# Binding the S5 work of a step behind that step's gate passes, and giving the v steps more of it than the z_b steps

## The chip, the cores and the metric

The kernel runs on one core of one Trainium2 chip. The metric is the device time of one execution in microseconds; lower is better. The engines are TensorE (PE, matrix products into PSUM), VectorE (DVE), ScalarE (ACT), GpSimd (POOL), and SyncE (SP), whose queue issues the DMAs. Each engine runs its own list of instructions in the order in which it was written down when the kernel was compiled.

## The reference

One layer of a bidirectional encoder trunk over a prompt of 1024 positions and a sample of 2048, width 1024, all in float32:

```
h = rmsnorm(x) ;  u, v, z_a, x_b, z_b = split(h @ w_in)          # 5 x 1024 columns
# branch A: gated MLP over chunks of 128 positions, 4 heads of 256
vh  = layernorm(gelu(v))
sv  = einsum('hpq,ncqhd->ncphd', w_s, vh) + b_s                  # 128 x 128 mixing
y_a = gelu(u) * sv * silu(z_a)
# branch B: S5, 64 groups of 16 channels, 64 complex states, forward and backward
s_t = a * s_(t-1) + B x_t ;  y = Re(C s) + d_skip * x            # scans over time
gy  = gelu(y) ;  y_b = gy * sigmoid(gy @ w_glu + b_glu) * silu(z_b)
out = rmsnorm(x + concat(y_a, y_b) @ w_out)
```

## The kernel before, in words

Every large product is made of three matmuls (`mm3`, lines 59 to 61), since each operand is held as a rounded high part and a low rest. Making the two parts is a `split`: a copy on ScalarE, then a subtraction on VectorE or GpSimd. The positions are worked on in three blocks of 1024 (`th`), each in two halves (`jh`).

The kernel has a first stage (norm, x_b columns, S5 tables), a middle stage, and a last one (the GLU product and the output projection). The change lies in the middle stage. There, for each block in the order 2, 0, 1, come three loops of *steps*. A step is one half's product with one slab of weights, and its *gate*, the passes that empty its PSUM bank:

- 16 **v steps** (`v_part`): 48 matmuls of 256 columns, then, in every second of them, a Gelu on ScalarE; for the odd column blocks also batch statistics on VectorE (L507).
- 16 **z_b steps** (`zb_op`): 24 matmuls of 512 columns, then a tanh on ScalarE (L527) and a multiply on VectorE (L528). Beside them stand 8 small matmuls of the position mixing (`mix`, tile `sv`, L484 and L485), their two passes (L488, L489), and the normalisation and split of the next chunk of v (`norm_chunk` L465, `split_chunk` L472 and L473).
- 32 **u and z_a steps** (`u_op`, `za_op`): 24 matmuls of 512 columns each; u has a Gelu on ScalarE (L566) and two passes on VectorE (L563, L568), z_a a tanh (L527) and two passes on VectorE (L528, L577).

PSUM holds five banks under the tag `mm`; the products of all three kinds and `sv` share them. The weights of a sweep of two steps (tile `whl`) are double buffered; in the first block they are split on ScalarE (L151) and GpSimd (L152) and written to DRAM, in the other two they are loaded again from there.

After each step the program calls `advance`, which adds 0.5 to a counter `done[0]` and takes from the generator `s5_groups` as many *half groups* of the S5 branch as 128 x `done[0]` / 92 asks for (`TOT` is 92, of 96 in all; the S5 work ends eight units of counter before the middle stage does). The two halves of a group g are:

- the first, `states(g)`: 6 matmuls (tile `pb`), two products with the tables (L1094, L1095), two sums, two scans over time (L1102, tile `gt`), two products (L1107, L1108), two sums (L1109, L1110), the split of `h` (ScalarE copy and VectorE subtraction, L1036 and L1037). Then the splits for group g+1 (`prepare`) and, for even g, the first part of two groups' tables (`tables`), for odd g the last part (`finish_tables`: a VectorE pass L1055, an abs L1056 and a sine L1058 on ScalarE). The sine lies in another table of ScalarE's functions than tanh and Gelu, so that a table load stands on either side of it.
- the second: `outputs(g-1)`: 9 matmuls (tile `py`) and a Gelu (L1127); `decay(g+1)`, a ScalarE pass that writes the factor `dec` of the next group's scan (L1116) into its only buffer; `issue(g+2)`, the loads of a later group on SP's queue.

The order in which each engine runs its instructions is not the order of the source. A planner works it out at compile time with a model of durations: of the instructions that its model finds ready it takes the one with the highest priority, and priority goes by the place in the source, with `tc.high_priority` moving the gates ahead by 100 places. So it may set S5 work that the source places after a step ahead of that step's gate, where the model finds the engine free.

Of the kernel before, what the change touches and what calls it, by code (L numbers as in the profile page):

```python
# [24 lines left out]
J = 8  # L25
NTH = 3
KK = NTH * P
GRP = 64
# [35 lines left out]
def hybrid_encoder(ctx, tc, a, outs):  # L64
# [117 lines left out]
    def sweep(pool, half, ops, after, hp=WHP):  # L182

        ws = [ready.pop(0) for _ in ops]
        for jh in range(2):
            for w, f in zip(ws, ops):
                ps = pool.tile([P, 512], F32, tag="mm", name="mm")
                h = half(jh)
                for kt in range(KT):
                    mm3(nc, ps, w[:, 0, kt], w[:, 1, kt], h[kt][:, 0], h[kt][:, 1], kt == 0, kt == KT - 1)  # L190
                if jh:
                    next_w(hp)
                f(jh, ps)
                after()
# [5 lines left out]
    def cols(t):  # L200
        return t.rearrange("p (k j) -> p j k", j=J)
# [161 lines left out]
    with ExitStack() as p2:  # L363
# [5 lines left out]
        ps_mm = p2.enter_context(tc.tile_pool(name="ps_mm2", bufs=5, space=PSUM, reuse_waits="tile"))  # L369
        ps_b = p2.enter_context(tc.tile_pool(name="ps_b", bufs=1, space=PSUM))  # L370

        s5 = s5_groups(nc, spool, ps_b, small, kio, f8h, f8l, r8, xb_d, ks_d, mat_d, gy_d)
        done = [0, 0]
        wg, g0 = [], []

        def stage_tile(name):
# [24 lines left out]
                    g0.append((gf, gh))  # L401

        late = [[], []]

        def flush():

# [4 lines left out]
        def advance(n=0.5):  # L411

            flush()
            done[0] += n
            if done[1] == 2 * GRP and done[0] % 1 == 0:
                preload()
            while done[1] < min(2 * GRP, 2 * GRP * done[0] / TOT):
                next(s5)
                done[1] += 1

        def get_half(hf):
# [15 lines left out]
        for th in (2, 0, 1):  # L437
# [53 lines left out]
            def v_part(acc, w, cb, q, jh):  # L491

                for cc in range(2):
                    ps = acc[jh][cc]
                    for i in range(2):
                        csl = slice(P * (2 * cc + i), P * (2 * cc + i) + P)
                        for t in range(4):
                            h, wh, wl = hs[jh][4 * q + t], w[:, 0, 2 * t:2 * t + 2], w[:, 1, 2 * t:2 * t + 2]

                            mm3(nc, ps[:, i], h[:, 0, csl], h[:, 1, csl], wh, wl, q == t == i == 0, q == i == 1 and t == 3)  # L500
                    if q:
                        c = slice(2 * cc, 2 * cc + 2)
                        sl = slice(256 * cb, 256 * cb + 256)
                        with tc.high_priority(offset=HP):
                            S.activation(vs[jh][:, c, sl], ps, AF.Gelu_apprx_tanh)
                            for i in (2 * cc, 2 * cc + 1) if cb % 2 else ():
                                V.bn_stats(sts[jh][:, i, cb // 2], vs[jh][:, i, 512 * (cb // 2):256 * cb + 256])  # L507
                advance()

            for cb in range(4):  # L510
                acc = [[ps_mm.tile([P, 2, 256], F32, tag="mm", name="acc") for _ in range(2)] for _ in range(2)]
# [12 lines left out]
            def gate(t, jh, ps):  # L524

                o = by_j(t, jh)
                S.activation(o, cols(ps), AF.Tanh, scale=0.5)  # L527
                V.scalar_tensor_tensor(o, o, 1.0, cols(ps), op0=ALU.add, op1=ALU.mult)  # L528

            def store(dst, fb, t):  # L530
                x = dst[J * th:J * th + J, :, fb].rearrange("j p k -> p j k"), t
# [7 lines left out]
            def zb_op(fb, jh, ps):  # L539
                if not jh:  # L540
                    mix(fb, 0)
                    if fb < KT - 1:
                        norm_chunk(fb + 1)
                        split_chunk(fb + 1, 0)
                    zs[0] = stage_tile("zb").rearrange("p (j k) -> p j k", j=J)
                with tc.high_priority(offset=HP):
                    gate(zs[0], jh, ps)
                if jh:
                    mix(fb, 1)
                    if fb < KT - 1:  # L550
                        split_chunk(fb + 1, 1)
                    store(zb_d, fb, zs[0])

            for fb in range(KT):
                sweep(ps_mm, lambda jh: hs[jh], [lambda *x: zb_op(fb, *x)], advance)

            def part(fb, jh):
                return vs[jh][:, :, P * fb:P * fb + P]

            def u_op(fb, jh, ps):  # L560
                t = part(fb, jh)
                with tc.high_priority(offset=HP):
                    V.scalar_tensor_tensor(t, t, LG[:, fb:fb + 1], RB[:, fb:fb + 1].to_broadcast([P, 4, P]),  # L563
                                           op0=ALU.mult, op1=ALU.add)
                with tc.high_priority(offset=HP):
                    S.activation(ps, ps, AF.Gelu_apprx_tanh)  # L566
                    t = t.rearrange("p c (j k) -> p c j k", j=J)
                    V.tensor_tensor(t, t, ps.rearrange("p (c k j) -> p c j k", c=4, j=J), op=ALU.mult)  # L568

            def za_op(fb, jh, ps):  # L570
                if not jh:
                    zs[1] = stage_tile("za").rearrange("p (j k) -> p j k", j=J)
                with tc.high_priority(offset=HP):
                    gate(zs[1], jh, ps)
                    o = by_j(zs[1], jh)
                    o = o.rearrange("p j (c k) -> p j c k", c=4)
                    V.tensor_tensor(o, o, part(fb, jh).rearrange("p c (j k) -> p j c k", j=J), op=ALU.mult)  # L577
                if jh:
                    store(ya_d, fb, zs[1])
                    if th != 1 and fb == KT - 1:  # L580
                        hs[1] = get_half((2 * th + 3) % 6)
                elif th != 1 and fb == KT - 1:
                    hs[0] = get_half((2 * th + 2) % 6)
# [429 lines left out]
    finish(*last)  # L1013


def s5_groups(nc, sp, ps, small, kio, f8h, f8l, r8, xb_d, ks_d, mat_d, gy_d):


    V, S, G, T = nc.vector, nc.scalar, nc.gpsimd, nc.tensor
    dma = nc.sync.dma_start  # L1020
    sh = [P, 2, KK]
# [11 lines left out]
        V.memset(keep[64:128, c:c + 1], 0.0)  # L1033

    def split(t, src, eng):
        S.copy(t[:, 0], src)  # L1036
        eng.tensor_tensor(t[:, 1], src, t[:, 0].bitcast(F32), op=ALU.subtract)  # L1037

    def tables(g):

# [42 lines left out]
    def states(g):  # L1083
        u, mi, mo = st[g]
        tb = st.pop(("tab", g))
        cs = tb[:, 0:1].to_broadcast(sh)
        sn = tb[:, 1:2].to_broadcast(sh)

        pb = ps.tile([P, 2, 512], F32, tag="pb", name="pb")[:, :, 0:KK]
        for i in range(2):  # L1090
            mm3(nc, pb[:, i], mi[:, 0, i], mi[:, 1, i], u[:, 0], u[:, 1], True, True)
        b1 = sp.tile(sh, F32, tag="b1", name="b1")
        b2 = sp.tile(sh, F32, tag="b2", name="b2")
        V.tensor_tensor(b1, pb, cs, op=ALU.mult)  # L1094
        V.tensor_tensor(b2, pb[:, ::-1], sn, op=ALU.mult)  # L1095
        V.tensor_tensor(b1[:, 0], b1[:, 0], b2[:, 0], op=ALU.add)
        V.tensor_tensor(b1[:, 1], b1[:, 1], b2[:, 1], op=ALU.subtract)
        dec = st.pop(("dec", g))
        bf = b1.rearrange("p i k -> p (i k)")
        for r, o, z in ((slice(0, 64), gp[:, 2:2 * KK + 2], (0, P)), (slice(64, 128), gp[:, 0:2 * KK], (P - 1, KK - 1))):  # L1100
            f = slice(None, None, 1 if r.start == 0 else -1)
            V.tensor_tensor_scan(o[r, f], dec[r, f], bf[r, f], 0.0, op0=ALU.mult, op1=ALU.add)  # L1102
            V.memset(gt[r, :, z[0]:z[1] + 1:z[1] - z[0]], 0.0)
        h = sp.tile([P, 2] + sh[1:], F32R, tag="h", name="h", bufs=2)
        h1 = sp.tile(sh, F32, tag="b1", name="h1")
        h2 = sp.tile(sh, F32, tag="b2", name="h2")
        V.tensor_tensor(h1, gt, cs, op=ALU.mult)  # L1107
        V.tensor_tensor(h2, gt[:, ::-1], sn, op=ALU.mult)  # L1108
        V.tensor_tensor(h1[:, 0], h1[:, 0], h2[:, 0], op=ALU.subtract)  # L1109
        V.tensor_tensor(h1[:, 1], h1[:, 1], h2[:, 1], op=ALU.add)  # L1110
        split(h, h1, V)
        st[g] = u, mo, h

    def decay(g):
        dec = sp.tile([P, 2 * KK], F32, tag="dec", name="dec")
        S.activation(dec.rearrange("p (i k) -> p i k", i=2), keep.unsqueeze(1).to_broadcast(sh), AF.Copy,  # L1116
                     scale=r8[:, g:g + 1])
        st["dec", g] = dec
# [25 lines left out]
    for g in range(GRP):  # L1144
        states(g)
        store()
        if g < GRP - 1:
            prepare(g + 1)
        if g % 2 == 0 and g < GRP - 2:
            tables(g + 2)  # L1150
        if g % 2 == 1 and g < GRP - 1:
            finish_tables(g + 1)
        yield
        if g:
            outputs(g - 1)
        if g < GRP - 1:
            decay(g + 1)
        if g < GRP - 2:
            issue(g + 2)
        if g == GRP - 1:  # L1160
            store()
            outputs(g)
            store()
        yield
# [30 lines left out]
```

## Time and profile before

| | |
|---|---|
| time, median of 3 runs | 2592.8 us (2588.3 to 2597.44) |
| the profiled execution | 2590.47 us |
| its span, first to last instruction | 2588.7 us |
| TensorE busy | 2465.0 us |
| VectorE, ScalarE, GpSimd busy | 1745.0, 999.5, 608.2 us |
[...]

The span is of one execution with the hardware profiler on. A busy TensorE is one with a matmul in flight; lower clock shows as longer matmuls, not as idle time. The middle stage's steps run from about 398 to 1783 us of the span: the first block's v, z_b and u/z_a from 398.5, 504.0 and 649.9 us, the z_b of the other two from 994.9 and 1454.0.

### The profile page before, as it was taken

Reading aid. Unit: us, or ns where it says so; the run is one execution under the profiler, and the core shown is the slowest. Engines: PE = TensorE matmul, PEld = TensorE weight load, DVE = VectorE, ACT = ScalarE, POOL = GpSimd, SP = SyncE. Lnnn points to the kernel's source line nnn. Section 1 sums busy time; section 2 is a strip of 40 time slices with the busy share of each in tenths; the row PEclk is TensorE's granted clock in tenths of the full one; section 3 lists DMA queues with packets and bytes.
Section 4 is the critical chain, followed back from the end, with each engine's and each line's share of the span. In section 5 each row is a group of like instructions: output and inputs, shape, how many; then the busy total and the mean of one; then the engine's idle time right before and its main releaser. Section 6 shows DMA issues by size and latency. Waiting matters only on the chain.

```text
span 2588.7 us, 34059 instructions
## 1 busy us (share of the span) xinstructions
PE 2465.0 (95%) x12313; PEld 2090.5 (81%) x12313; DVE 1745.0 (67%) x2890; ACT 999.5 (39%) x1729; POOL 608.2 (23%) x623
## 2 busy tenths in 40 slices
PE   6899999998999799999989989999999999999998
PEld 4777779877887698888879978888888888888887
DVE  6888857888988888888887989874344433333332
ACT  5343344455445444545444354422223311111110
POOL 1579863434322312211021221001000200000000
PEclk9999999999999899999999999999999999999999
DMA  8565554434554533444453344446565732222220
GB/s 233 168 190 145 148 159 168 165 120 153 166 172 148 188 125 124 128 132 132 147 171 121 125 130 133 132 146 195 148 183 152 228 110 95 97 94 98 98 74 33
DMA packets 363017, 367.21 MB, mean 142 GB/s; under 512 B 40768, under 2 KB 308576, under 8 KB 350560
## 3 DMA queue, kind: packets, MB, share of 16 engines
q1 hardware_dynamic: 311008, 343.99, 41.9%
q10 hardware_dynamic: 51840, 21.04, 3.4%
q8 instruction: 97, 1.59, 0.3%
q14 instruction: 72, 0.59, 0.1%
HBM read 229.76 MB, written 135.20 MB: 141 GB/s over the span
## 4 chain that ended last, share of the span: by engine, by line
PE 57%; DVE 20%; ACT 4%; DMA 3%; issue 3%; POOL 2%; SPq 0%; ACTq 0%; DVEq 0%; POOLq 0%
PE mm L59 15%; PE mm L60 15%; PE mm L61 15%; DVE gt L1102 4%; PE acc L61 3%; PE acc L59 3%; PE acc L60 3%; DVE h L1108 1%; DVE h L1107 1%; DVE b L1095 1%; DMA whl<-wc_d 1%; DMA hf<-hs_d 1%; DVE u L1037 1%; DVE tab L1048 1%; DVE b L1094 1%
## 5 line engine op out<-in xcount | busy, mean ns | idle before, releaser
L59 PE MATMUL mm<-w,yh 128*128 128x512 f32 x768 | 302.5, 394 | 0.0
L60 PE MATMUL mm<-w,yh 128*128 128x512 f32 x768 | 301.9, 393 | 0.0
L61 PE MATMUL mm<-w,yh 128*128 128x512 f32 x768 | 301.3, 392 | 0.0
L59 PE MATMUL mm<-ha,whl 128*128 128x512 f32 x704 | 281.2, 400 | 18.1 <-ACT whl L151 10.3
L61 PE MATMUL mm<-ha,whl 128*128 128x512 f32 x704 | 278.0, 395 | 2.5 <-POOL whl L152 2.3
L59 PE MATMUL mm<-hb,whl 128*128 128x512 f32 x704 | 278.5, 396 | 0.0
L60 PE MATMUL mm<-ha,whl 128*128 128x512 f32 x704 | 278.0, 395 | 0.0
L60 PE MATMUL mm<-hb,whl 128*128 128x512 f32 x704 | 276.7, 393 | 0.0
L61 PE MATMUL mm<-hb,whl 128*128 128x512 f32 x704 | 276.5, 393 | 0.0
L152 POOL TENSOR_TENSOR whl<-wf,whl 128x512 fp32r<-128x512 f32 x112 | 168.4, 1519 | 272.7 <-ACT whl L151 258.5
L1102 DVE TENSOR_TENSOR_SCAN gt<-dec,b 64x768 f32<-64x768 f32 x128 | 229.9, 1796 | 3.8
L1116 ACT ACTIVATE dec<-keep,r 128x768 f32<-128x768 uint8 x64 | 60.1, 938 | 314.2 <-DVE gt L1102 314.2
L59 PEld LDWEIGHTS mm<-ha,whl 128*128 128x128 f32 x704 | 134.3, 191 | 47.5 <-ACT whl L151 12.0
L61 PEld LDWEIGHTS mm<-w,yh 128*128 128x128 f32 x768 | 144.2, 188 | 33.9
L59 PEld LDWEIGHTS mm<-w,yh 128*128 128x128 f32 x768 | 144.2, 188 | 33.3
L60 PEld LDWEIGHTS mm<-w,yh 128*128 128x128 f32 x768 | 144.0, 187 | 33.0
L681 DVE SCALAR_TENSOR_TENSOR yh<-yf,yh 128x512 fp32r<-128x512 f32 x96 | 66.8, 699 | 146.7 <-ACT yh L680 96.8
L1037 POOL TENSOR_TENSOR mo<-m,mo 128x384 fp32r<-128x384 f32 x64 | 79.0, 1234 | 366.9 <-ACT mo L1036 358.5
L61 PEld LDWEIGHTS mm<-ha,whl 128*128 128x128 f32 x704 | 134.1, 191 | 33.5 <-POOL whl L152 5.3
L710 DVE TENSOR_TENSOR xr<-xr,mm 128x512 f32<-128x512 f32 x48 | 33.0, 687 | 183.8 <-PE mm L61 183.8
L61 PEld LDWEIGHTS mm<-hb,whl 128*128 128x128 f32 x704 | 133.7, 190 | 28.2
L60 PEld LDWEIGHTS mm<-ha,whl 128*128 128x128 f32 x704 | 134.4, 191 | 26.7 <-DVE ha L285 1.1
(242 smaller groups left out, 6026.3 us busy)
## 6 DMA issues: line engine op xcount, KB each, us to landing
whl<-wc_d SPq DMA_DIRECT2D x64, 1024.0 KB
wc_d<-whl SPq DMA_DIRECT2D x32, 1024.0 KB
wf<-in_w_in_dram SPq DMA_DIRECT2D x112, 256.0 KB
m<-mat_d SPq DMA_DIRECT2D x128, 128.0 KB
xb_d<-xo SPq DMA_DIRECT2D x24, 512.0 KB
U<-xb_d SPq DMA_DIRECT2D x64, 192.0 KB
gy_d<-gy SPq DMA_DIRECT2D x64, 192.0 KB
zb_d<-zb SPq DMA_DIRECT2D x24, 512.0 KB
```

Of the source, the lines that this page charges most:

```text
L59: nc.tensor.matmul(out, lh, rh, start=first, stop=False)
L60: nc.tensor.matmul(out, lh, rl, start=False, stop=False)
L61: nc.tensor.matmul(out, ll, rh, start=False, stop=last)
L152: G.tensor_tensor(flat[:, 1, sl], wf, flat[:, 0, sl].bitcast(F32), op=ALU.subtract)
L681: V.scalar_tensor_tensor(y[:, 1], yf, sc, y[:, 0].bitcast(F32), op0=ALU.mult, op1=ALU.subtract)
L710: V.tensor_tensor(x, x, t.ps[i], op=ALU.add)
L1037: eng.tensor_tensor(t[:, 1], src, t[:, 0].bitcast(F32), op=ALU.subtract)
L1048: V.scalar_tensor_tensor(fr, kio, f8l[:, g + q:g + q + 1], fr, op0=ALU.mult, op1=ALU.add)
L1094: V.tensor_tensor(b1, pb, cs, op=ALU.mult)
L1095: V.tensor_tensor(b2, pb[:, ::-1], sn, op=ALU.mult)
L1102: V.tensor_tensor_scan(o[r, f], dec[r, f], bf[r, f], 0.0, op0=ALU.mult, op1=ALU.add)
L1116: S.activation(dec.rearrange("p (i k) -> p i k", i=2), keep.unsqueeze(1).to_broadcast(sh), AF.Copy, scale=r8[:, g:g + 1])
```

## The change

Three things are done. First, each gate pass is remembered in a dictionary `tail`, one entry for ScalarE and one for VectorE, and every S5 half group that `advance` takes is traced inside `tc.issue_after` of these entries: its instructions on ScalarE come in ScalarE's list after the last gate pass traced there, and likewise on VectorE. Such an edge is an order in one engine's list and no wait on a semaphore. Second, inside the S5 generator `decay(g+1)` is bound in the same way behind the ScalarE copy of the split of `h` of group g. Third, `advance` is called with 0.66 after a v step and 0.34 after a z_b step; a u or z_a step keeps 0.5. The later preloads for the last stage are counted by calls instead of by whole units, which gives the same every second call.

```
+        tail = {}
...
             flush()
             done[0] += n
-            if done[1] == 2 * GRP and done[0] % 1 == 0:
+            done[2] += 1
+            if done[1] == 2 * GRP and done[2] % 2 == 0:
                 preload()
             while done[1] < min(2 * GRP, 2 * GRP * done[0] / TOT):
-                next(s5)
+                with ExitStack() as behind:
+                    for i in tail.values():
+                        behind.enter_context(tc.issue_after(i.ins))
+                    next(s5)
                 done[1] += 1
...
-                            S.activation(vs[jh][:, c, sl], ps, AF.Gelu_apprx_tanh)
+                            tail["S"] = S.activation(vs[jh][:, c, sl], ps, AF.Gelu_apprx_tanh)
...
-                advance()
+                advance(0.66)
...
-                S.activation(o, cols(ps), AF.Tanh, scale=0.5)
-                V.scalar_tensor_tensor(o, o, 1.0, cols(ps), op0=ALU.add, op1=ALU.mult)
+                tail["S"] = S.activation(o, cols(ps), AF.Tanh, scale=0.5)
+                tail["V"] = V.scalar_tensor_tensor(o, o, 1.0, cols(ps), op0=ALU.add, op1=ALU.mult)
...
-                sweep(ps_mm, lambda jh: hs[jh], [lambda *x: zb_op(fb, *x)], advance)
+                sweep(ps_mm, lambda jh: hs[jh], [lambda *x: zb_op(fb, *x)], lambda: advance(0.34))
...
+                    tail["S"] = S.activation(ps, ps, AF.Gelu_apprx_tanh)
+                    tail["V"] = V.tensor_tensor(t, t, ps.rearrange("p (c k j) -> p c j k", c=4, j=J), op=ALU.mult)
+                    tail["V"] = V.tensor_tensor(o, o, part(fb, jh).rearrange("p c (j k) -> p j c k", j=J), op=ALU.mult)
...
-        split(h, h1, V)
+        st["hi"] = split(h, h1, V)
...
         if g < GRP - 1:
-            decay(g + 1)
+            with tc.issue_after(st["hi"].ins):
+                decay(g + 1)
```

## Rows read from the trace of the kernel before

**Rows 1.** The page, busy time of TensorE: us, share of the span, instructions.

```profile
PE 2465.0 (95%) x12313; PEld 2090.5 (81%) x12313; DVE 1745.0 (67%) x2890; ACT 999.5 (39%) x1729; POOL 608.2 (23%) x623
```

**Rows 2.** Windows by stage: length, PE, PEld, DVE, ACT, POOL busy, granted clock.

```profile
398.50:504.00 105.50, 105.10 (x841) 104.64 (x840) 85.20 (x111) 49.12 (x80) 38.46 (x29) 1.00 0.52 176
504.00:649.90 145.90, 127.07 (x595) 108.85 (x594) 131.58 (x188) 78.15 (x142) 59.75 (x44) 0.93 0.44 140
649.90:877.70 227.80, 211.59 (x936) 175.68 (x934) 200.98 (x245) 111.48 (x180) 69.88 (x54) 0.97 0.51 165
...
994.90:1122.40 127.50, 121.70 (x596) 104.95 (x594) 110.88 (x187) 68.53 (x123) 34.44 (x28) 0.96 0.41 129
...
1454.00:1582.00 128.00, 118.30 (x598) 102.09 (x597) 113.98 (x172) 63.39 (x116) 32.75 (x27) 1.00 0.41 126
```

**Rows 3.** Windows of three stretches of the second block: v, z_b, u/z_a.

```profile
915.40:994.94 79.54, 79.54 (x637) 79.54 (x637) 62.00 (x92) 35.95 (x57) 7.91 (x8) 1.00 0.35 117
1015.88:1059.47 43.59, 43.59 (x223) 37.88 (x223) 36.19 (x63) 25.96 (x48) 12.51 (x10) 1.00 0.44 137
1205.95:1295.32 89.37, 89.37 (x413) 76.20 (x412) 73.89 (x104) 42.08 (x62) 8.37 (x9) 1.00 0.44 139
```

**Rows 4.** Waits of TensorE, 398 to 1783 us: total us, times, longest.

```profile
PE sv L484 <- DVE zb L528: 19.3, 9, 5.0
PE mm L59 <- ACT whl L151: 10.3, 4, 6.5
...
PE sv L484 <- ACT vh L472: 6.1, 2, 4.3
```

**Rows 5.** Waits of ScalarE, the same stretch.

```profile
ACT dec L1116 <- DVE gt L1102: 314.2, 61, 12.2
...
ACT h L1036 <- DVE h L1110: 87.6, 48, 5.0
```

**Rows 6.** Waits of VectorE, the same stretch.

```profile
DVE za L528 <- ACT za L527: 44.5, 15, 5.7
...
DVE v L568 <- ACT mm L566: 37.6, 14, 4.6
DVE zb L528 <- ACT zb L527: 30.1, 9, 4.8
```

**Rows 7.** Timeline of ScalarE from 606.5 us, a z_b step: start, duration.

```profile
610.62 0.94 ACT L1116 ACTIVATE dec<-keep,r 128x768 f32<-128x768 uint8 x1 [7.06 <-DVE gt L1102]
611.47 0.58 ACT L527 ACTIVATE zb<-mm 128x512 f32<-128x512 f32 x1
```

**Rows 8.** Timeline of TensorE at the same step.

```profile
613.02 0.57 PE L484 MATMUL sv<-wsT,vh 128*128 128x256 f32 x1 [4.10 <-DVE v L489]
```

**Rows 9.** Timeline of ScalarE from 743 us, a z_a step.

```profile
751.24 0.85 ACT L1056 ACTIVATE tab<-tab 128x768 f32<-128x768 f32 x1 [3.50 <-DVE tab L1055]
...
753.40 1.58 ACT L1058 ACTIVATE tab<-tab,qpi 128x1536 f32<-128x1536 f32 x1
755.00 1.28 ACT L527 ACT_TABLE_LOAD   x1
756.30 0.60 ACT L527 ACTIVATE za<-mm 128x512 f32<-128x512 f32 x1
```

**Rows 10.** Timeline of VectorE at the same step.

```profile
756.93 0.69 DVE L528 SCALAR_TENSOR_TENSOR za<-za,mm 128x512 f32<-128x512 f32 x1 [4.85 <-ACT za L527]
```

**Rows 11.** Groups of VectorE, second block's u/z_a stage: total us, mean ns.

```profile
L1107 DVE TENSOR_TENSOR h<-gt,tab 128x768 f32<-128x768 f32 x11 | 10.5, 958 | 0.3
...
L1110 DVE TENSOR_TENSOR h<-h,h 128x384 f32<-128x384 f32 x11 | 6.9, 624 | 0.0
```

**Rows 12.** Groups of VectorE, first v stage.

```profile
L507 DVE BATCH_NORM_STATS2 st<-v 128x6 f32<-128x512 f32 x14 | 9.1, 684 | 3.2 <-ACT v L505 3.2
```

**Rows 13.** One line's instructions, a table pass: ns least, median, most.

```profile
L1048 DVE SCALAR_TENSOR_TENSOR tab<-kio,f8l,tab x64: 558/614/1655, 378.1 to 1666.0; 128x384 f32<-128x384 f32 x64
```

**Rows 14.** Timeline of VectorE from 546 us, a z_b step.

```profile
546.66 5.10 DVE L465 TENSOR_SCALAR v<-v,rvy,nb 128x1024 f32<-128x1024 f32 x3
```

More of the change, by code (lines that the diff above doesn't have):

```diff
@@ L370, in hybrid_encoder @@
         ps_b = p2.enter_context(tc.tile_pool(name="ps_b", bufs=1, space=PSUM))
-        s5 = s5_groups(nc, spool, ps_b, small, kio, f8h, f8l, r8, xb_d, ks_d, mat_d, gy_d)
-        done = [0, 0]
+        s5 = s5_groups(tc, spool, ps_b, small, kio, f8h, f8l, r8, xb_d, ks_d, mat_d, gy_d)
+        done = [0, 0, 0]
         wg, g0 = [], []
@@ L565, in u_op @@
                 with tc.high_priority(offset=HP):
-                    S.activation(ps, ps, AF.Gelu_apprx_tanh)
+                    tail["S"] = S.activation(ps, ps, AF.Gelu_apprx_tanh)
                     t = t.rearrange("p c (j k) -> p c j k", j=J)
-                    V.tensor_tensor(t, t, ps.rearrange("p (c k j) -> p c j k", c=4, j=J), op=ALU.mult)
+                    tail["V"] = V.tensor_tensor(t, t, ps.rearrange("p (c k j) -> p c j k", c=4, j=J), op=ALU.mult)
             def za_op(fb, jh, ps):
@@ L576, in za_op @@
                     o = o.rearrange("p j (c k) -> p j c k", c=4)
-                    V.tensor_tensor(o, o, part(fb, jh).rearrange("p c (j k) -> p j c k", j=J), op=ALU.mult)
+                    tail["V"] = V.tensor_tensor(o, o, part(fb, jh).rearrange("p c (j k) -> p j c k", j=J), op=ALU.mult)
                 if jh:
@@ L1013, in s5_setup, with s5_groups @@
     finish(*last)
-def s5_groups(nc, sp, ps, small, kio, f8h, f8l, r8, xb_d, ks_d, mat_d, gy_d):
+def s5_groups(tc, sp, ps, small, kio, f8h, f8l, r8, xb_d, ks_d, mat_d, gy_d):
+    nc = tc.nc
     V, S, G, T = nc.vector, nc.scalar, nc.gpsimd, nc.tensor
@@ L1035, in split @@
     def split(t, src, eng):
-        S.copy(t[:, 0], src)
+        hi = S.copy(t[:, 0], src)
         eng.tensor_tensor(t[:, 1], src, t[:, 0].bitcast(F32), op=ALU.subtract)
+        return hi
     def tables(g):
```

## The prediction

> **What bounds the kernel now.** I read the page first: TensorE is busy for 2465.0 of 2588.7 us, so 124 us are to be had in all [rows 1]. The windows by stage then say where those 124 us lie. The projections of the middle stage run from 398 to 1783 us, in three blocks of 64 steps: 16 v steps, 16 z_b steps, 32 u/z_a steps. To know what a stage would take if TensorE never waited, I looked for stretches in which its busy time equals the window and the clock is 1.00 [rows 3]. The first holds 12 v steps and 4 S5 groups (12x48 + 4x15 = 636 matmuls, 637 counted): 6.63 us a step. The second holds 6 z_b steps and 2 groups: 7.27 us. The third holds 14 u/z_a steps and 5 groups: 6.38 us. At that pace a z_b stage takes 16 x 7.27 = 116 us and a u/z_a stage 32 x 6.38 = 204 us.
>
> [...] The first v stage takes 105.5 us, just its pace of 106. So the loss sits in z_b and in the first block's u/z_a, and v has none, with VectorE busy for only 85.2 of its 105.5 us against 131.6 of 145.9 in z_b.
>
> What TensorE waited for there is the gate's last pass on VectorE (the sv bank is not free) and, in u/z_a, the split of the next weights on ScalarE [rows 4]. Neither pass is long; both are late, and the waits of the two engines say why. ScalarE stood 314 us, 61 times, at the `dec` pass, which may not write before the scan of the group ahead is done, and another 88 us at the split of `h` [rows 5]. VectorE in turn stood 112 us (44.5 + 37.6 + 30.1) for a gate's ScalarE pass [rows 6]. Two scenes show one such wait each. At 610.6 us `dec` ends 7.06 us of standing, and the tanh of a z_b step starts right behind it [rows 7]; TensorE had stood 4.10 us when the next sv matmul starts [rows 8]. At 751 us the abs, a table load, the sine and another table load run ahead of a tanh that starts at 756.3 [rows 9], while VectorE stands 4.85 us for that tanh [rows 10]. That sine belongs to `finish_tables` of an odd group whose share is traced two steps later; the planner took it because it found it ready, though a gate was due.
>
> **The change, part by part.**
>
> *Issue behind the gate.* It adds no instruction and no semaphore: an edge between two instructions of one engine is only their order. It binds the ScalarE and VectorE instructions of a share; its matmuls, its DMAs on SP's queue and its splits on GpSimd get no edge of their own, but most of them read what those engines write and so come no earlier. What it takes away is work of a coming share ahead of a gate: the chain of abs, load, sine, load, 0.85 + 1.28 + 1.58 + 1.28 = 5.0 us [rows 9]. What is late next is that sine itself. It is needed two half groups later, 2/0.696 = 2.9 steps or 18 us at 6.38, and takes 5 us: covered. If the cover goes, the first product on VectorE waits and not TensorE, which asks for the `h` of a group three half groups after its start.
>
> *`dec` behind the split of `h`.* `dec` (0.94 us) then no longer stands at the head while the scans run. It is wanted by the next group's scans one group on, 18 us later in u/z_a and 15 in v, so its lateness is hidden. Behind it now stands the split of `h` itself, which waits for two products and two sums of VectorE more: 2 x 0.95 + 2 x 0.6, about 3.1 us [rows 11]. Queued behind it on ScalarE are gates, `vh` copies and weight splits, and TensorE waits for these. How often the planner still sets a gate behind that split no row of before shows. The bounds: never (the full 314 us of standing goes), or always (each wait grows by 3.1 us). I take a quarter of the removable loss as staying.
>
> [...]
>
> *Uneven shares.* 128 half groups over 92 units are 1.39 a unit: 0.696 half groups a step at 0.5, 0.918 at 0.66, 0.473 at 0.34. A block still gets 16 x 0.66 + 16 x 0.34 + 32 x 0.5 = 32 units, so TensorE's work only moves: 16 x 0.223 = 3.6 half groups, 1.8 groups, from each z_b to the v before it. On VectorE a group costs about 12.7 us in the first v stage: 85.2 busy, less 9.1 of batch statistics [rows 12], over 6 groups. So z_b loses 23 us of VectorE work: 131.6 - 23 = 109 in 116, which fits where it did not. v gains them: 16 x 0.918 / 2 = 7.3 groups x 12.7 + 9 = 102 us in a stage that grows by the 1.8 x 15 = 27 matmuls that come with them, at the third stretch's mean of 89.37/413 = 0.216 us about 6 us, to 112. That is 91%, the share at which z_b now stumbles (131.6 of 145.9 is 90%); but v has no VectorE pass between TensorE and a free bank, only a Gelu. I charge 2 us a block, 6 in all; the bounds are 0, and the excess of the second rival.
>
> In the first block, passes on VectorE stretch when GpSimd splits weights and `vh`: L1048 takes 0.614 us at the median and 1.655 at most [rows 13]. [...] That speaks against moving passes into the first v stage; what it would make of the time is the v rival below.
>
> *What stays.* The wait of 4.3 us at the start of the first z_b for `vh` [rows 4] and the three normalising passes of 5.10 us ahead of a gate [rows 14] are no S5 work. With the slow clock behind them I leave 14 us in the first z_b and 3.4 in the second. On SP's queue the loads of a later group wait until a split has freed their buffer; with later splits they come later, and weights queue behind them. I cost it at nothing, as weights are staged a sweep of two steps (13 us) ahead; uncovered it costs what they come late beyond that. `preload` comes on every second call as before.
>
> **The sum.** Removable in z_b: (29.6 - 14) + (11.2 - 3.4) + 11.7 = 35 us, of which I take three quarters, 26. In the first u/z_a 23.5 are lost, but VectorE is busy 201.0 us there against 204 at pace, so I take 10. Less 6 in v: 30 us. The profiled execution took 2590.5 us (span 2588.7 and 1.8 around it), 2.3 below the median of 2592.8: 2590.5 - 30 = 2560 us.
>
> **The rivals.**
> 1. The wait only changes its name: the split of `h` holds the gates where `dec` did. For it: it already made ScalarE stand 88 us. Against it: z_b has a third less S5 work to be held by. Gain and loss cancel: about 2588 us. Chance 0.13.
> 2. VectorE becomes the bound in v. A v step of 112/16 = 7.0 us gives a group 2/0.918 steps, 15.3 us, of which 9.1/7.3 = 1.2 go to statistics. From 14.1 us a group on, VectorE falls behind and TensorE comes to wait for `h`. At 14.8 us (12.7 and the stretch of two passes like that of rows 13) it loses 0.7 x 7.3 = 5 us a block; if the Gelus of v stick behind the split of `h` too, each group costs its 3.1 us more, 23. Three blocks give up to 84; half of that against z_b's 26, with nothing won in u/z_a, is 2590 + 42 - 26 = 2606 us. [...] Against it: TensorE reads `h` three half groups after the start, 22 us. Chance 0.15.
> 3. All the removable loss goes: 35 + 23.5 = 58 us, 2532 us. Chance 0.15.
>
> My forecast of 2560 has 0.57. Faster is the forecast and the third, 0.72; same is the first, 0.13; slower 0.15. (About 0.3%, 8 us, is what a measurement of this kernel can tell from no change.) The range takes the third's end, 2532, and the first, and stops at 2598 short of the second, leaving out about 0.17. The forecast's own range is 2545 to 2576.
>
> **What the profile after would show.** Right: ScalarE's standing at `dec` falls from 314 us to under 60; VectorE's for gates falls from 112 to under 50; z_b stages near 116 to 122 us less the 6 us that moved, v near 112 to 114, the first u/z_a near 215; the split of `h` shows more standing than 88 us. Wrong: a v stage over 118 us with TensorE waiting for `h` or for a bank of `acc` (second rival), or gates in z_b still late with the split of `h` ahead of them (first). What would also break it: the planner's whole order shifts with such edges, and a weight load issued late on SP costs more than I allow.

## The result, and the profile after

The changed kernel takes 2553.55 us (median of 4 runs, 2552.49 to 2554.4), the kernel before in the same runs 2593.88 us: a ratio of 0.9846 [0.9828, 0.9865], 40 us less. The profiled execution took 2554.4 us against 2590.47. TensorE was busy 2465.0 us of 2588.7 before [rows 1]; the page's line on the engines gives 2453.2 of 2552.6 after. So of 36.1 us of span, 24.3 are idle time of TensorE and 11.8 its busy time, for the same 12313 matmuls.

```profile
PE 2453.2 (96%) x12313; PEld 2087.7 (82%) x12313; DVE 1705.5 (67%) x2890; ACT 990.7 (39%) x1726; POOL 602.9 (24%) x623
```

Where the time went is read from the windows, one for each stage of the three blocks (v, z_b, u/z_a), with the columns of [rows 2].

```profile
399.50:513.80 114.30, 111.41 (x862) 110.69 (x862) 96.74 (x121) 57.46 (x92) 35.27 (x28) 0.97 0.50 165
513.80:647.30 133.50, 119.71 (x578) 102.23 (x578) 112.59 (x180) 67.12 (x129) 53.93 (x41) 0.95 0.44 144
647.30:851.80 204.50, 202.94 (x930) 171.97 (x928) 184.10 (x236) 110.24 (x175) 68.16 (x53) 1.00 0.55 182
851.80:976.90 125.10, 117.28 (x882) 115.92 (x883) 110.49 (x149) 62.75 (x103) 27.40 (x23) 0.96 0.43 141
976.90:1099.20 122.30, 115.13 (x564) 98.40 (x564) 95.14 (x169) 54.05 (x104) 30.36 (x24) 0.96 0.40 126
1099.20:1304.30 205.10, 205.00 (x945) 174.61 (x944) 165.85 (x239) 99.07 (x154) 23.57 (x24) 1.00 0.45 146
1304.30:1429.50 125.20, 114.77 (x873) 113.64 (x874) 109.75 (x156) 63.97 (x100) 24.93 (x20) 0.96 0.44 141
1429.50:1548.20 118.70, 116.12 (x573) 99.81 (x573) 98.16 (x167) 55.71 (x106) 30.58 (x24) 0.97 0.40 128
1548.20:1746.80 198.60, 197.28 (x898) 166.51 (x898) 136.11 (x195) 73.07 (x116) 17.42 (x16) 1.00 0.44 141
```

The table below sets stage lengths side by side, for every kernel of this study. Each is the distance between the first matmuls of two stages in the timeline, so one may differ from a rounded window by a us. Outside this middle stage nothing changed (1204.6 us before, 1205.2 after).

| kernel | v | z_b | u/z_a | sums v / z_b / u and z_a | middle stage |
|---|---|---|---|---|---|
| before | 105.6 117.3 118.9 | 145.9 127.4 128.1 | 227.8 212.7 200.4 | 341.7 / 401.5 / 640.9 | 1384.1 |
| after | 114.3 125.1 125.2 | 132.5 122.3 118.7 | 205.5 205.0 198.7 | 364.6 / 373.6 / 609.2 | 1347.4 |
| tail_only | 104.7 119.5 122.6 | 133.6 121.7 128.0 | 204.6 205.3 198.7 | 346.8 / 383.3 / 608.6 | 1338.6 |
| dec_only | 105.1 117.9 119.0 | 144.0 128.0 129.1 | 230.0 219.7 199.1 | 342.0 / 401.1 / 648.9 | 1392.0 |
| shares_only | 114.8 126.2 123.7 | 134.4 118.6 122.9 | 227.8 212.0 200.3 | 364.7 / 375.9 / 640.1 | 1380.7 |
| order_only | 104.7 119.3 121.9 | 133.5 121.5 127.0 | 205.5 205.2 199.0 | 345.9 / 382.1 / 609.7 | 1337.8 |
| act_tail | 104.7 118.9 120.4 | 132.8 123.5 129.0 | 206.1 204.8 198.8 | 344.0 / 385.3 / 609.7 | 1339.0 |
| dve_tail | 105.8 118.5 123.6 | 134.1 123.0 124.2 | 214.1 205.7 198.8 | 347.9 / 381.3 / 618.6 | 1347.7 |
| v_taper | 110.8 122.9 122.7 | 130.4 117.3 121.3 | 205.5 205.2 198.8 | 356.5 / 369.0 / 609.5 | 1335.0 |
| u_more | 104.7 126.4 121.5 | 129.6 118.6 118.7 | 211.9 207.4 201.4 | 352.5 / 366.9 / 620.7 | 1340.1 |
| sine_bound | 104.7 115.4 122.7 | 138.6 123.0 124.2 | 216.0 204.8 198.6 | 342.7 / 385.8 / 619.5 | 1348.0 |
| all_but_sine | 104.7 121.1 120.3 | 140.6 126.0 132.2 | 225.0 204.8 198.7 | 346.1 / 398.8 / 628.6 | 1373.5 |
| taper_even | 108.2 119.9 120.9 | 133.6 117.7 125.8 | 205.5 205.1 198.8 | 349.1 / 377.1 / 609.4 | 1335.6 |
| tail_shares | 114.8 124.2 126.5 | 132.2 119.4 117.3 | 204.6 205.1 198.7 | 365.5 / 368.9 / 608.5 | 1342.8 |

From before to after, v and z_b together gave 5 us (743.2 to 738.2): work moved from one to the other. The gain is u/z_a's, 31.7 us, of which 22.3 in the first block, where TensorE's granted clock also went from 0.97 to 1.00, and 7.7 in the second.

The waits of ScalarE from 398 to 1760 us, the view of [rows 5]:

```profile
ACT h L1044 <- DVE h L1119: 294.5, 59, 13.1
ACT zb L534 <- PE mm L61: 86.8, 25, 5.9
ACT mm L573 <- PE mm L61: 75.1, 24, 4.9
ACT za L534 <- PE mm L61: 74.0, 25, 5.9
```

ScalarE stands hardly less: it is idle for 734.6 us of the middle stage before and 703.9 after (the windows' lengths less its busy time). The pass `dec` has no row any more, and the split of `h` has 294.5 us in its place. The three lower rows are the gates: ScalarE now stands ready before TensorE has finished the bank. VectorE's waits, the view of [rows 6]:

```profile
DVE zb L535 <- ACT zb L534: 59.7, 19, 5.1
DVE za L535 <- ACT za L534: 48.9, 26, 4.9
DVE v L575 <- ACT mm L573: 43.8, 24, 4.8
```

VectorE's standing for gates rose from 112.2 to 152.4 us in a faster kernel. In [rows 6] such a wait meant a late ScalarE; here ScalarE itself waits for TensorE, and a VectorE with its other work done stands behind it. The same row reads in opposite ways, and only the row of the engine it waits for tells which.

A measure that tells the two apart is the lateness of the gates: for each of the 144 z_b, u and z_a steps, the start of ScalarE's gate pass less the end of the step's last matmul, both from the timeline.

| kernel | median lateness, us | steps late by over 3 us | late in all, us |
|---|---|---|---|
| before | 4.15 | 80 | 630 |
| dec_only | 3.27 | 76 | 620 |
| shares_only | 2.03 | 64 | 507 |
| all_but_sine | 1.44 | 52 | 418 |
| sine_bound | 1.25 | 41 | 358 |
| dve_tail | 1.31 | 46 | 341 |
| tail_only | 0.08 | 34 | 235 |
| after | 0.04 | 28 | 198 |
| act_tail | 0.09 | 21 | 174 |

The measure leaves out v and its way to the first `vh` of z_b: the changed kernel is late by less than tail_only, and takes 8 us longer.

What TensorE still waits for, the view of [rows 4]:

```profile
PE sv L490 <- ACT vh L478: 15.8, 3, 7.0
PE acc L61 <- DVE hb L437: 7.1, 2, 3.9
PE acc L59 <- ACT ha L436: 5.9, 3, 2.8
PE sv L490 <- DVE zb L535: 5.3, 3, 3.5
...
PE mm L59 <- ACT whl L151: 0.7, 1, 0.7
```

The gate's last VectorE pass costs 5.3 us where it cost 19.3, the split of weights 0.7 where it cost 10.3. But the wait for the first `vh` of a z_b stage grew from 6.1 to 15.8 us.

### The profile page after: what moved, and what is told of

It reads as the page before. It is cut to its first block, busy times and chain, and to the rows that moved or that the text cites. A ratio compares the mean times of both kernels' runs of the same rounds, so it can differ in the third digit from the quotient of the medians.

```text
span 2552.6 us, 33954 instructions
## 1 busy us (share of the span) xinstructions
PE 2453.2 (96%) x12313; PEld 2087.7 (82%) x12313; DVE 1705.5 (67%) x2890; ACT 990.7 (39%) x1726; POOL 602.9 (24%) x623
## 4 chain that ended last, share of the span: by engine, by line
PE 67%; DVE 15%; ACT 2%; issue 2%; POOL 2%; DMA 1%; DVEq 0%; ACTq 0%; SPq 0%; POOLq 0%
PE mm L61 20%; PE mm L59 20%; PE mm L60 20%; DVE gt L1111 4%; DVE st L513 1%; DVE h L1117 1%; PE sv L490 1%; PE py L59 1%; PE py L61 1%; PE py L60 1%; DVE b L1103 1%; DVE b L1104 1%; DVE h L1116 1%; DVE tab L1056 1%; DVE tab L1057 1%
## 5 line engine op out<-in xcount | busy, mean ns | idle before, releaser
L59 PE MATMUL mm<-ha,whl 128*128 128x512 f32 x704 | 277.4, 394 | 2.2 <-DVE ha L284 0.9
L61 PE MATMUL mm<-ha,whl 128*128 128x512 f32 x704 | 275.3, 391 | 0.6 <-POOL whl L152 0.6
L60 PE MATMUL mm<-ha,whl 128*128 128x512 f32 x704 | 275.3, 391 | 0.0
L1045 POOL TENSOR_TENSOR mi<-m,mi 128x256 fp32r<-128x256 f32 x64 | 57.9, 904 | 579.5 <-ACT mi L1044 566.6
L1044 ACT CAST h<-h 128x768 fp32r<-128x768 f32 x64 | 53.4, 835 | 294.5 <-DVE h L1119 294.5
L61 PEld LDWEIGHTS mm<-hb,whl 128*128 128x128 f32 x704 | 133.5, 190 | 28.1
L61 PEld LDWEIGHTS mm<-ha,whl 128*128 128x128 f32 x704 | 132.6, 188 | 28.7 <-POOL whl L152 1.1
L59 PEld LDWEIGHTS mm<-ha,whl 128*128 128x128 f32 x704 | 132.6, 188 | 28.6 <-DVE ha L284 1.6
L60 PEld LDWEIGHTS mm<-hb,whl 128*128 128x128 f32 x704 | 134.0, 190 | 25.8 <-DVE hb L285 0.2
## 6 DMA issues: line engine op xcount, KB each, us to landing
m<-mat_d SPq DMA_DIRECT2D x128, 128.0 KB
```

Source lines behind the costliest of these rows:

```text
L59: nc.tensor.matmul(out, lh, rh, start=first, stop=False)
L60: nc.tensor.matmul(out, lh, rl, start=False, stop=False)
L61: nc.tensor.matmul(out, ll, rh, start=False, stop=last)
L1044: hi = S.copy(t[:, 0], src)
```

## The experiments

Each kernel was timed together with the kernel before on the same chip, and the ratio is to that. In kernels without the edges in `advance` (dec_only, shares_only, sine_bound, all_but_sine) line numbers are 2 lower than in the changed kernel.

**First four: the parts alone.** Is it the order behind the gates, the order of `dec`, or the shares?

*tail_only* keeps the order behind the gates, and undoes the rest:

```
-                advance(0.66)
+                advance(0.5)
...
-                ... lambda: advance(0.34))
+                ... lambda: advance(0.5))
...
-            with tc.issue_after(st["hi"].ins):
-                decay(g + 1)
+            decay(g + 1)
```

> Only the shares bound behind the gate passes of ScalarE and VectorE; dec is free, every step has 0.5. Theory 1 (the order and the shares each give part, as in the prediction): u/z_a of the first block falls from 228 us to about 210, z_b stays near 140, 125, 125; about 2575 us. Theory 2 (the order gives all of the gain; the shares only move work from z_b to v): the three u/z_a stages fall by about 33 us as in the changed kernel; 2550 to 2562 us. Theory 3 (dec is what blocks): dec still stands some 250 us at the head of ScalarE and the time stays within 8 us of 2594.

Measured: 2545.22 us against 2592.29, 0.9819 [0.9806, 0.9831]. One part of three gives 47 us, more than the whole change.

*dec_only* keeps only the order of `decay`: shares at 0.5, and the edges in `advance` gone:

```
-                    for i in tail.values():
-                        behind.enter_context(tc.issue_after(i.ins))
```

> Only decay bound behind the split of h; shares free to run ahead of gates, every step has 0.5. Theory 1: z_b of the second and third block falls by some 5 us each; about 2580 us. Theory 2: the sine chain still runs ahead of gates, so little is won: 2580 to 2594 us. Theory 3: nearly the whole gain, 2555 to 2565 us. If the split of h merely takes the place of dec, ScalarE's wait for it grows to about 300 us and the time stays at 2594.

Measured: 2597.52 us, 1.002 [1.0011, 1.0029]. The waits of its ScalarE, from 398 to 1790 us:

```profile
ACT h L1042 <- DVE h L1117: 235.1, 43, 11.8
ACT tab L1052 <- DVE h L1115: 176.0, 29, 9.7
```

The 314 us at `dec` [rows 5] are gone and stand at other passes, and 620 us of gates' lateness were 630 before. So the wait changed its place and the gates stayed late; what less standing would be worth this run doesn't tell.

*shares_only* keeps 0.66 and 0.34 without either order (both edits above that remove edges).

> Only 0.66 per v step and 0.34 per z_b step; no order bound. Theory 1: z_b shrinks by 26 us beyond what moves, v loses 6, so about 2574 us. Theory 2: v and z_b together stay what they were or get worse (in the changed kernel v grew by 23 us and z_b shrank by 27), so 2588 to 2600 us.

Measured: 2584.66 us, 0.9972 [0.9963, 0.9981]. z_b gives 25.6 us, v takes 23.0 of them back, u/z_a doesn't change.

*order_only* keeps both orders, with shares of 0.5.

> Both orders bound, every step at 0.5. Theory 1: without the uneven shares about 20 us of the gain are missing: 2570 to 2575 us. Theory 2: the gain is whole or larger, 2540 to 2556 us, as the first sv matmul of a z_b stage no longer waits 7 us for a VectorE that is behind.

Measured: 2543.81 us, 0.9815 [0.9802, 0.9827]: as fast as tail_only, 10 us faster than the changed kernel. With the gates in order, the uneven shares cost time.

**Second four: which list, and why the shares cost.** The first two are tail_only with edges in one engine's list alone:

```
-                    for i in tail.values():
+                    for i in [tail[e] for e in 'S' if e in tail]:
```

for *act_tail*, and `'V'` for *dve_tail*.

> As tail_only, but the shares are bound on ScalarE alone. If ScalarE's list is what made the gates late (sine chain, table passes, splits ahead of tanh and Gelu), the whole gain stays: 2543 to 2552 us. If the order of VectorE's passes matters as much, half of it: 2560 to 2575 us.

Measured: 2545.29 us against 2595.0, 0.9812 [0.9799, 0.9826].

> As tail_only, but the shares are bound on VectorE alone. The sine chain begins with a VectorE pass (the first line of finish_tables), so this order holds the sine back too. If the sine chain is the culprit, the gain stays nearly whole: 2545 to 2555 us. If it is ScalarE's other passes (first table passes, splits, dec), most of the gain is gone: 2575 to 2592 us.

Measured: 2552.74 us, 0.9841 [0.9827, 0.9854]. ScalarE's list alone gives everything, VectorE's alone most. The two are not independent: the chain of the sine begins with a VectorE pass (L1064 after the change), so binding that pass holds the sine back too. What VectorE's list misses is in the first u/z_a, 214.1 us against 206.1.

*v_taper* is the changed kernel with the shares cut where v goes over into z_b: 12 v steps at 0.66, the last 4 at 0.3, and z_b at 0.43. (It so changes two shares at once; taper_even below leaves z_b's alone.)

```
-                advance(0.66)
+                advance(0.3 if cb == 3 else 0.66)
...
-                ... lambda: advance(0.34))
+                ... lambda: advance(0.43))
```

> The changed kernel, but the last four v steps of a block take 0.3 and the z_b steps 0.43, so that a block has its 32 units. If the uneven shares cost their 10 us at the change from v to z_b, where the last Gelu of v stands behind the split of h, the first sv wait of about 7 us shrinks to 3 and the time is 2541 to 2547 us. If v is slow through its rate of S5 work as such, 2550 to 2554 us.

Measured: 2542.49 us, 0.9797 [0.9784, 0.981], 11 us below the changed kernel by the medians; TensorE's wait for `vh` falls from 15.8 us to 3.4. What the last v shares do is seen at the first `vh`. It is a copy of the first chunk of v's first half, and waits for that half's last Gelu (of the 15th of 16 v steps) and then, all on VectorE, for the half's statistics (L513, L455), a dozen small passes that make the scale of them (the last is L460), and the normalisation (L471). ScalarE's timeline of the changed kernel (start, duration, engine, line, operation, and in brackets the idle time before it with what ended that):

```profile
505.62 0.60 ACT L511 ACTIVATE v<-acc 128x512 f32<-128x512 f32 x1 [2.28 <-PE acc L61]
...
518.39 0.84 ACT L1044 CAST h<-h 128x768 fp32r<-128x768 f32 x1 [7.71 <-DVE h L1119]
519.13 0.93 ACT L1125 ACTIVATE dec<-keep,r 128x768 f32<-128x768 uint8 x1
519.96 0.57 ACT L511 ACTIVATE v<-acc 128x512 f32<-128x512 f32 x1
...
525.89 1.14 ACT L478 CAST vh<-v 128x512 fp32r<-128x512 f32 x2
```

VectorE's:

```profile
512.15 1.76 DVE L1111 TENSOR_TENSOR_SCAN gt<-dec,b 64x768 f32<-64x768 f32 x1
513.97 0.06 DVE L1112 MEMSET gt<- 64x4 f32 x1
514.06 1.29 DVE L513 BATCH_NORM_STATS2 st<-v 128x6 f32<-128x512 f32 x2
...
523.55 0.72 DVE L460 SCALAR_TENSOR_TENSOR nb<-mv,rvy 128x4 f32<-128x4 f32 x1
524.19 0.94 DVE L1103 TENSOR_TENSOR b<-pb,tab 128x768 f32<-128x768 f32 x1
525.06 1.52 DVE L471 TENSOR_SCALAR v<-v,rvy,nb 128x1024 f32<-128x1024 f32 x2
```

and TensorE's, of the same kernel:

```profile
526.56 0.80 PE L490 MATMUL sv<-wsT,vh 128*128 128x256 f32 x2 [6.95 <-ACT vh L478]
```

The first half's last Gelu runs on time, at 505.62 us. Its statistics start only at 514.06 and the normalisation at 525.06, and VectorE shows no idle time between: products, sums and two scans of the S5 work stand in its list ahead of these passes and among them. (On ScalarE the sine stands ahead of `vh` as well, but it ends at 525.80, the normalisation at 525.86.) From the end of the 15th step's matmuls to the start of the first `vh` it takes 20.3, 20.1 and 15.0 us in the three blocks of the changed kernel; 16.4, 12.2 and 8.1 in order_only, where a v step takes 0.5; and 16.2, 12.0 and 6.7 in v_taper. In the first block TensorE stands 6.95, 3.2 and 3.4 us for it in these three.

The Gelu at 519.96 us shows what a wait on ScalarE holds up: the last matmul of v ends at 512.92, but the Gelu stands behind the split of `h`, which waits 7.71 us for VectorE. It belongs to the other half, though, and the first `vh` doesn't need it. In the second block the first half's last Gelu does stand so, 4.4 us; in the third it doesn't. The first `vh` of v_taper, ScalarE:

```profile
519.15 1.14 ACT L478 CAST vh<-v 128x512 fp32r<-128x512 f32 x2 [3.34 <-DVE v L471]
```

There too it is VectorE's normalisation that comes last.

*u_more* is tail_only with the work moved the other way, out of z_b into u/z_a: v 0.5, z_b 0.4, u/z_a 0.55.

```
-                        sweep(ps_mm, lambda jh: hs[jh], [op], advance)
+                        sweep(ps_mm, lambda jh: hs[jh], [op], lambda: advance(0.55))
...
-                    sweep(ps_mm, lambda jh: hs[jh], ops, advance)
+                    sweep(ps_mm, lambda jh: hs[jh], ops, lambda: advance(0.55))
```

> tail_only with the S5 work moved the other way: 0.5 per v step, 0.4 per z_b step, 0.55 per u or z_a step. If what z_b still loses (some 30 us over three blocks against its pace) comes from a VectorE with too much to do there, 2533 to 2540 us, since u/z_a is at TensorE's pace with VectorE busy for 81% in the second block. If it comes from normalising passes and the start of the stage, no change: 2543 to 2547 us. If u/z_a has no room, it grows by over 10 us.

Measured: 2544.9 us, 0.981 [0.9797, 0.9824]. z_b gives 16.4 us and u/z_a takes 12.1, v 5.7: moved work without a gain beyond tail_only.

**Last four: the sine, and the best version.** *sine_bound* is the kernel before with one edge, for `finish_tables` alone:

```
         if g % 2 == 1 and g < GRP - 1:
-            finish_tables(g + 1)
+            with ExitStack() as behind:
+                for i in tail.values():
+                    behind.enter_context(tc.issue_after(i.ins))
+                finish_tables(g + 1)
```

> The kernel before, with finish_tables alone (VectorE pass, abs, sine) bound behind the gate passes; all other S5 work may run ahead, 0.5 per step. If the sine chain ahead of the gates is the cause of the loss, most of the 47 us come back: 2545 to 2560 us. If the cause is S5 work ahead of gates in general (first table passes, the scans and products of VectorE, dec), little comes: 2575 to 2594 us.

Measured: 2554.71 us against 2595.55, 0.9847 [0.9833, 0.986]. Three passes of every second group (one on VectorE, the abs and the sine), put behind the gate with the sine's table loads, give as much as the whole change, though ScalarE goes on standing at `dec`:

```profile
ACT dec L1123 <- DVE gt L1109: 226.5, 49, 10.8
ACT h L1042 <- DVE h L1117: 106.4, 50, 4.2
```

*all_but_sine* is its counterpart, tail_only with `finish_tables` left free and everything else of a share bound:

```
+        with ExitStack() as behind:
+            for i in tail.values():
+                behind.enter_context(tc.issue_after(i.ins))
             states(g)
...
         if g % 2 == 1 and g < GRP - 1:
             finish_tables(g + 1)
```

> tail_only with finish_tables left free. If the sine chain is the cause: 2575 to 2594 us. If it is S5 work in general: 2545 to 2560 us. If both runs land half way, the two add up.

Measured: 2577.41 us, 0.9934 [0.9922, 0.9947]. Alone 41 us and 18 us, together 47: they overlap by 12, and the sine is the larger.

*tail_shares* is the changed kernel with `decay` left free.

> The changed kernel with decay left free. If binding dec behind the split of h costs at the change from v to z_b (ScalarE stands 7.7 us there with dec and the last Gelu behind the split), 2544 to 2549 us. If the split of h alone holds that Gelu, no change: 2551 to 2556 us.

Measured: 2550.91 us, 0.9829 [0.9816, 0.9842]. The interval overlaps that of the changed kernel (0.9846 [0.9828, 0.9865]); if the order of `dec` does anything there, it costs. It overlaps that of tail_only (0.9819) as well, so what the uneven shares cost without the order of `dec` is not clear of the noise.

*taper_even* is both orders with 0.6 in the first 12 v steps, 0.2 in the last 4, and 0.5 elsewhere, so z_b keeps its share and only the end of v is emptied.

```
-                advance(0.66)
+                advance(0.2 if cb == 3 else 0.6)
...
-                ... lambda: advance(0.34))
+                ... lambda: advance(0.5))
```

> Both orders bound; 0.6 in the first twelve v steps of a block, 0.2 in the last four, 0.5 elsewhere: the block's v steps keep 8 units in all. Against order_only (2543.8 us) only the end of v has less S5 work in hand. If what z_b still loses at its start is VectorE's and ScalarE's lag from v, 2534 to 2541 us; if not, 2542 to 2546 us.

Measured: 2540.82 us, 0.9792 [0.9779, 0.9806]: the fastest median, and its interval lies below that of the changed kernel. TensorE's waits have no row for `vh` any more (10.5, 6.4 and 6.4 us from the 15th step to `vh`), so the S5 work at the end of v is what made that wait. That the kernel also beats v_taper or order_only the intervals don't show: its first z_b still takes 133.6 us.

## Why the time came out near the forecast, by its steps

The forecast was 30 us of gain; the profiled executions differ by 36.1, the middle stage by 36.7. The sum held, its terms did not: v and z_b together were to give 26 - 6 = 20 and gave 5, u/z_a was to give 10 and gave 31.7. Two errors cancelled, so that the time came out so near is luck.

**What bounds the kernel.** The places were right: z_b and the first u/z_a, where gates ran late. The losses that the sum counts with, 29.6, 11.2 and 11.7 us in z_b and 23.5 in the first u/z_a, are the windows of [rows 2] (145.90, 127.50, 128.00 and 227.80 us) less the paces of 116.3 and 204.3 that [rows 3] give. The second block's u/z_a was overlooked. It stood at 212.7 us where the pace of [rows 3] makes 204, and is now at 205.0. That v loses nothing was read from the first v alone: the other two took 117.3 and 118.9 us, where their pace is 106. At their starts TensorE waits for the splits of the next halves (`ha` and `hb`), 13.0 us in the changed kernel.

**Issue behind the gate.** Right, and the whole of the gain (tail_only 0.9819). The scene of [rows 9], an abs, two loads and a sine ahead of a ready tanh, was the main loss: binding that chain alone gives 41 us. That its lateness is covered was right too: TensorE's largest waits after hold none for `h` of more than 2.1 us. Here is a scene of the first u/z_a after, ScalarE's timeline:

```profile
746.80 0.60 ACT L534 ACTIVATE za<-mm 128x512 f32<-128x512 f32 x1 [2.93 <-PE mm L61]
...
755.43 0.84 ACT L1044 CAST h<-h 128x768 fp32r<-128x768 f32 x1 [6.56 <-DVE h L1119]
756.17 0.93 ACT L1125 ACTIVATE dec<-keep,r 128x768 f32<-128x768 uint8 x1
757.00 0.58 ACT L573 ACTIVATE mm<-mm 128x512 f32<-128x512 f32 x1
```

ScalarE waits 2.93 us for TensorE to fill the first bank; the next gate still stands behind 6.56 us of waiting for `h`, and here that costs little: the whole stage is within 1.5 us of its pace.

**`dec` behind the split of `h`.** This step failed. The prediction read ScalarE's 314 us of standing as time that gates lost, and let a quarter of the removable loss hang on where it goes. dec_only moves it to other passes and gains nothing (1.002); sine_bound leaves 226.5 us of it at `dec` and gains 41. The first rival described this part rightly, the wait changed its name (88 to 294.5 us at the split of `h`); its price was wrong for the same reason, since 294.5 us of standing at `h` go with a kernel 40 us faster. A waiting pass did hold a ready one: the Gelu at 519.96 us above could have run from 512.92 and stood behind the split of `h`. But the rival's time doesn't follow from that: who stands behind a wait did matter, 18 to 47 us in these runs (all_but_sine, tail_only).

**Uneven shares.** The work moved about as worked out, 17.5 us of matmuls in three blocks, and v grew by 18.7 from order_only to after. VectorE's busy time in the first z_b fell from 131.6 us to 112.6 (109 worked out), and the first v took 114.3 us (112 to 114). What failed is that z_b gave back only 8.5 us of the 17.5. TensorE's waits in z_b for VectorE (`zb` L535 and `v` L495) are 16.4 us in order_only and 6.0 after, so the shares did help there; but those for the first `vh` are 3.2 and 15.8, and the granted clock of the second z_b, which now starts with such a wait of 6.96 us, went from 1.00 to 0.96. The second rival had VectorE falling behind in v, and it does; but TensorE pays for it neither at `h` nor at a bank of v, but at `vh`, where v ends. Whether VectorE's 90% busy is why z_b stumbled stays open: the first z_b takes 132.5 us at 84% (112.59 of 133.50) and 133.5 in order_only at 92% (122.59 of 133.50), but the one starts with 6.95 us of waiting and the other with 3.2. Shares helped where gates were late (shares_only, 8 us) and cost 10 where they were not.

**The cap on the first u/z_a.** This step failed most: 23.5 us were lost and 10 were taken, since VectorE was busy 201.0 us of a pace of 204. It is busy 184.1 us after, for nearly the same work (236 records, 245 before). Three groups of VectorE in that stage, before (columns: form, count, then busy us and mean ns of one, then idle before):

```profile
L577 DVE TENSOR_TENSOR za<-za,v 128x512 f32<-128x512 f32 x15 | 17.6, 1176 | 0.1
L1037 DVE TENSOR_TENSOR u<-U,u 128x384 fp32r<-128x384 f32 x11 | 11.2, 1015 | 0.9 <-ACT u L1036 0.9
L1110 DVE TENSOR_TENSOR h<-h,h 128x384 f32<-128x384 f32 x11 | 10.1, 918 | 0.0
```

and after:

```profile
L584 DVE TENSOR_TENSOR za<-za,v 128x512 f32<-128x512 f32 x15 | 14.1, 937 | 0.5
L1045 DVE TENSOR_TENSOR u<-U,u 128x384 fp32r<-128x384 f32 x11 | 9.2, 838 | 0.0
L1119 DVE TENSOR_TENSOR h<-h,h 128x384 f32<-128x384 f32 x11 | 6.0, 548 | 0.0
```

The same passes, as many of them, take 17 to 40% less, and these three groups make 9.6 of the 16.9 us. A busy time that holds stretched passes is no floor. Nor did the whole gain need them shorter: in sine_bound VectorE is busy 199.3 us in this stage, and it takes 216.0, 11.8 less than before; the other 10.5 came together with the shorter passes, and no run parts them. With this stage and the second block's at their pace, the third rival was right for u/z_a and wrong for z_b.

**What stays.** 14 and 3.4 us were to stay in the first two z_b and none in the third. How much of the 14 is the slow clock was the author's estimate, and no run shows it apart. Measured is the granted clock of the first z_b: 0.93 before [rows 2], with 0.51 from 514 to 519 us, behind 5 us of which TensorE was busy for 0.83; and 0.95 after. With shares of 0.5 (order_only), 133.5, 121.5 and 127.0 us against 116 leave 17.5, 5.5 and 11.0: the order alone took 19.4 us out of z_b, where the forecast counted on 26 from the whole change. Of what is left, waits for the first `vh` (3.2), the gate's passes (10.0) and one mixing pass (L495, 6.4) are seen, at a clock of 0.95 in the first; whether another order of the normalisation removes them wasn't tried.

**The signs named beforehand.** Right: `dec`'s standing gone, the first v at 114.3, the split of `h` above 88 us. The other two v stages, at 125.1 and 125.2, are over the 118 us that was to speak for the second rival, but started from 117.3 and 118.9, and TensorE waits for no bank of `acc`, and for `h` only 4.2 us in the whole middle stage. Wrong: z_b (132.5, 122.3, 118.7 for 110 to 116), the first u/z_a (205.5 for 215), and VectorE's standing for gates (152.4 for under 50): that sign was chosen wrongly, since it also grows when gates are on time.

## What to carry to other kernels

Price a wait by what stands behind it and is due, not by its own sum: take the distance from a bank's last matmul to the pass that empties it, step by step; moving 314 us of one engine's standing to other passes was worth nothing here, and three passes taken from ahead of the gates 41 us. When work is bound behind gates, look at the changes between stages, where a chain of small passes of one feeds the first product of the next, and keep other work small just there. Before taking an engine's busy time for a floor, see in the trace whether its passes are stretched: VectorE's 201.0 us in the first u/z_a became 184.1 for nearly the same work.

## What the runs showed of the hardware beyond this

VectorE's time for one pass of the same shape went with what GpSimd did meanwhile: 0.55 us for a sum of `h` with GpSimd at rest, up to 1.64 beside a split. The sum of `h` in the first u/z_a has a mean of 918 ns before and 548 ns after, with GpSimd busy 69.88 and 68.16 us there, so it isn't less work on GpSimd. It is which passes meet. Two of the eleven before, on VectorE:

```profile
726.14 1.64 DVE L1110 TENSOR_TENSOR h<-h,h 128x384 f32<-128x384 f32 x1
744.36 0.55 DVE L1110 TENSOR_TENSOR h<-h,h 128x384 f32<-128x384 f32 x1
```

and GpSimd at the first of them, splitting weights:

```profile
724.51 2.86 POOL L152 TENSOR_TENSOR whl<-wf,whl 128x512 fp32r<-128x512 f32 x2 [6.53 <-ACT whl L151]
```

The four of the eleven that take 1.36 to 1.64 us all run beside a split on GpSimd; of the other seven, at 0.55 us, six run beside no pass of GpSimd. After the change none of the eleven meets one, and all take 0.54 to 0.55 us. So it is with the table pass of [rows 13]: of its 64 passes the 50 beside which GpSimd rests take 0.62 us at most, and of the 14 others 11 take 0.98 to 1.66.
